# Building half of a scatter's key tiles one phase earlier, shares per phase for gathered rows, and ten whole blocks instead of six

## The chip, the cores and the metric

The kernel runs on one NeuronCore of a Trainium2 chip, as one launch. The metric is the device time of one execution in microseconds (us). Before the change the median of three runs is 2544.63 us (2541.19 to 2548.04).

## The reference, cut to what matters

Two layers of a hybrid decoder run over 256 prompt tokens and 64 sample tokens, in fp32 with 1024 features. The first half of a layer (retention and a recurrent branch) is not touched here. The second half is PEER: every token has eight heads, each head picks the best 16 of 128 x 128 experts by two lists of 128 keys, and each expert is one neuron.

```
q = (xf @ wq).reshape(n, 8, 2, 128);  s = einsum('nhpd,hpkd->nhpk', q, keys)
top_s, top_i = top_k(s, 16);  cand = top_s[:,:,0,:,None] + top_s[:,:,1,None,:]
best_s, best_c = top_k(cand.reshape(n, 8, 256), 16)
eidx = i1 * 128 + i2;  gate = softmax(best_s)          # 128 experts for each token
hid = gelu(einsum('nd,nkd->nk', x, u_tab[eidx])) * gate
out = einsum('nk,nkd->nd', hid, v_tab[eidx])
```

## The kernel before, in words

**Prompt tokens go through all 16384 experts as dense products.** A layer's expert half has eight phases of 32 items each, in the order U1, U0, U3, V1, U2, V0, V3, V2 (PHASES). The letter says which table is used and the digit which quarter of its 128 blocks. An item takes one block of 128 x 1024 fp32 numbers (512 KB), which SP loads into one of five `raw` buffers, five items ahead (`load`). `split`, two items ahead, has ACT round it to `hi` (L216) and DVE subtract to get `lo` (L218), in three buffers each, because a product is made as hi*hi + lo*hi + hi*lo in the fast fp32r format. A U item is 24 matmuls of 256 columns into PSUM, and after every second one a GELU into the SBUF tile `H`. A V item (`vmm`) is 12 matmuls of 512 columns that add to four PSUM banks held through all V phases. Its other operand is `H`, itself split by `hsplit` (L1146, L1147) once for two items. In V0 the items for which `whole` is true (i//2 in 3, 7, 11: six items) are not split. They multiply `raw` and `H` in plain fp32 (L1160), with four calls.

**The scatter turns the chosen experts into a dense weight on `H`.** It runs once for quarters 0 and 1 (f=0, during U3) and once for quarters 2 and 3 (f=1, during V0). Each time it takes 32 groups of eight tokens. A group needs a key tile `sA` (L1080: compare the first index with a ramp, 128 x 1024 in f16), a tile `sO` (L1083), a tile `sB` (L1085: times the gates), 16 matmuls of 64 columns (L1095, L1096) and one DVE operation on `H` (L1102). The scatter is a pipeline: step g builds group g, places group g-1 on TensorE and weighs group g-2. With f=0 each key tile is built and also stored to DRAM (`kept`), and with f=1 it is read back from there. `sA` has three buffers, `sB` and the PSUM bank two.

**Sample tokens take their experts by rows.** `sample()` gathers 64 row tiles of `peer_u` and then 64 of `peer_v` (one indirect DMA from POOL for each, L1223, 128 rows of 4 KB, 512 KB), in three buffers `g4`. DVE reduces or adds each one two steps later (L1232, L1246).

**The order is written out by generators.** `choose` (the top-16 work), `scatter` and `sample` yield a cost after each step. Twice in each item `background` adds half of the item's `budget` (TUNE["peer"], one number per phase) to a credit, and steps the queue `bg` until the credit is used up. Only what `bg` leaves goes to `bg2`, which holds `sample`. So in U3 and V0 rows are gathered when the scatter has ended, and in the other phases as fast as the budget allows (1.3 for a row). All five engines run their own instructions strictly in the order in which this program issues them, so a DVE instruction that waits for a gathered row holds up the next `lo`.

`phase` drains `choose` before U3 and a scatter before the V phase that needs it. `post_v2` drains what is left of both queues at item 28 of V2.

Of the kernel before, what the change touches and what calls it, by code (L numbers as in the profile page):

```python
# [12 lines left out]
F16 = mybir.dt.float16  # L13
# [4 lines left out]
OP = mybir.AluOpType  # L18
# [4 lines left out]
NPT = 256  # L23
# [27 lines left out]


TUNE = dict(gret=4.4, xr=3.6, grnn=1.6, ga=2.5, gb=3.1,
            peer=(1.45, 1.66, 2.5, 1.2, 1.2, 2.2, 1.2, 1.25))


class Background:
# [28 lines left out]
class Trunk:  # L86
# [134 lines left out]
    def run(self):  # L221
        self.items, self.blocks, self.raw, self.hl = [], [], {}, {}
        for l in range(self.depth):
            Layer(self, l).plan()
        self.credit = 0.0
        for k, it in enumerate(self.items):
            self.k = k
            if it.get("pre"):
                it["pre"]()
            self.split(k + 2)  # L230
            if not it["whole"]:
                self.load(k + RAWS)
            for _ in it["mm"](*self.hl.pop(k)):
                self.background(it, 0.5)
            if it["whole"]:
                self.load(k + RAWS)
            for f in self.late.pop(k, []):
                f()
            if it.get("post"):
                it["post"]()  # L240
            self.background(it, 0.5)
        self.final()

    def background(self, it, f):
        left = self.bg2.advance(self.bg.advance(self.credit + f * it["budget"]))
        self.credit = min(left, 0.0)

    def at(self, dk, f):
        self.late.setdefault(self.k + dk, []).append(f)
# [16 lines left out]
class Layer:  # L266
# [5 lines left out]
    def plan(self):  # L272
        T, a = self.T, self.a
        n0 = len(T.items)

        def add(mm, post=None, pre=None, lo="dve", budget=2.0, whole=False):
            T.items.append(dict(mm=mm, post=post, pre=pre, lo=lo, budget=budget, whole=whole))

        x = lambda: (T.xh, T.xl)
        pair = self.fm_pair(x)  # L280
        for c in range(8):
            add(pair[c] if c < 2 else self.fm(x), lambda c=c: self.post_qk(c), pre=self.start if c == 0 else None)
        for h in range(2):
            for kp in range(4):
                add(self.tm(x, h, kp), lambda h=h, kp=kp: self.post_v(h, kp))
        for c in range(8):
            add(self.fm(x), lambda c=c: self.post_gret(c), pre=self.start_ret if c == 0 else None, budget=TUNE["gret"])
        for c in range(8):
            add(self.fm(x), lambda c=c: self.post_xr(c), budget=TUNE["xr"])
        for c in range(8):  # L290
            add(self.fm(x), lambda c=c: self.post_grnn(c), pre=self.start_rgl if c == 0 else None, budget=TUNE["grnn"])
        for g in range(2):
            for c in range(8):
                add(self.fm(x), lambda g=g, c=c: self.post_gate(g, c), budget=TUNE[("ga", "gb")[g]])
        for c in range(8):
# [12 lines left out]
        for ph, (kind, q) in enumerate(PHASES):
            for i in range(PHB):
                e = q * PHB + i  # L310
                pre = (lambda kind=kind, q=q: self.phase(kind, q)) if i == 0 else None
                mm, post = (self.umm, self.post_u) if kind == "U" else (self.vmm, self.post_v2)
                add(mm(q, i), lambda post=post, q=q, i=i: post(q, i), pre=pre, budget=TUNE["peer"][ph],
                    whole=self.whole(kind, q, i))
                T.blocks.append(a["ut"][e] if kind == "U" else a["peer_v"].rearrange("(p j) d -> j p d", j=KEYS)[e])
        T.items[-1]["last"] = True
# [634 lines left out]
    def choose(self, t):  # L951
# [101 lines left out]
        T.at(3, turn)  # L1053
        yield 1.0

    def scatter(self, f):
        T, nc, pp = self.T, self.nc, self.pp
        ng = NPT // 8
        w2 = 2 * PHB
        st = {}  # L1060
        if f == 0:
            self.kept = [T.dp.tile([128, 1024], F16, tag=f"kept{g}", name="kept") for g in range(ng)]

        def v(t, g, w):
            pairs = t[:, g * 8:(g + 1) * 8].rearrange("p (a b) -> p a b", b=2)
            return pairs[:, :, None, :].to_broadcast([128, 4, w, 2])

        def ramp(k0, w):
            return T.iota_a[:, None, k0:k0 + w, :].to_broadcast([128, 4, w, 2])

        def fetch(g):
            A = st["A", g] = pp.tile([128, 4, 128, 2], F16, tag="sA", name="sA", bufs=3)
            if f:
                nc.sync.dma_start(A.rearrange("p a k b -> p (a k b)"), self.kept[g])

        def build(g):
            A = st.pop(("A", g))
            B = pp.tile([128, 2, 4, w2, 2], F16, tag="sB", name="sB", bufs=2)
            if f == 0:
                nc.vector.tensor_tensor(A, v(self.i1T, g, 128), ramp(0, 128), op=OP.is_equal)  # L1080
                nc.sync.dma_start(self.kept[g], A.rearrange("p a k b -> p (a k b)"))
            hot = pp.tile([128, 4, w2, 2], F16, tag="sO", name="sO")
            nc.vector.tensor_tensor(hot, v(self.i2T, g, w2), ramp(f * w2, w2), op=OP.is_equal)  # L1083
# [18 lines left out]
            nc.vector.scalar_tensor_tensor(hv, p, 1.0 / GSC, hv, op0=OP.mult, op1=OP.mult)  # L1102
            self.weighed[f] += 8

        if f:
            fetch(0)
        for g in range(ng + 2):
            while self.chosen < (1 if g < ng // 2 else 2):
                yield 2.0
            if g + f < ng:  # L1110
                fetch(g + f)
            if g < ng:
                build(g)
            if 0 <= g - 1 < ng:
                place(g - 1)
            if 0 <= g - 2 < ng:
                weigh(g - 2)
            yield 1.8 if f else 2.3

    def look_ahead(self, kind, q, i):  # L1120
        n = PHASES.index((kind, q)) + 1
# [26 lines left out]
            self.hid[q, i][2] = upto  # L1148

    def whole(self, kind, q, i):  # L1150
        return (kind, q) == ("V", 0) and i // 2 in (3, 7, 11)

    def vmm(self, q, i):
        nc, T = self.nc, self.T
# [250 lines left out]
```

## Time and profile before

| | before |
|---|---|
| median of 3 runs | 2544.63 us |
| profiled execution | 2543.64 us |
| its span | 2541.8 us |
| mean granted TensorE clock | 0.988 |
| expert half of layer 1, of layer 2 (to the end of V2) | 461.6 to 1267.9, 1728.0 to 2532.9 us |

Times below are from the span's start. Of a phase, the stretch runs from its first matmul to the first one of the next phase. Busy time is the time in which at least one instruction of the engine runs. On TensorE matmuls overlap, so a stretch with 100% is one in which it never stood still.

### The profile page before, as it was taken

How to read it: one execution, taken by the hardware profiler on the slowest of the kernel's cores; microseconds unless marked ns; L12 is line 12 of the kernel's file. 1: busy time of each engine (PE TensorE's matmuls, PEld its weight loads, DVE VectorE, ACT ScalarE, POOL GpSimd, SP SyncE). 2: the span in 40 equal slices, each digit the busy share in tenths (PEclk: the TensorE clock that was granted, in tenths of full speed). 3: DMA queues.
4: the chain of work that ended last, by engine and by line, in shares of the span. 5: the costliest groups of instructions: out<-in, count | busy, mean ns of one | idle time of the engine just before them, and what ended most of it. 6: DMA issues, size and time to landing. Idle time of an engine off the chain costs nothing. (4 is left out here: it accounts for less than half of the span.)

```text
span 2541.8 us, 42734 instructions
## 1 busy us (share of the span) xinstructions
PE 2422.8 (95%) x16588; PEld 2176.6 (86%) x16588; DVE 1955.1 (77%) x3503; ACT 1102.5 (43%) x1551; POOL 489.9 (19%) x305
## 2 busy tenths in 40 slices
PE   8989999999899999999999899999999999999998
PEld 7879899999898897777788798899998988977776
DVE  7465657887898878888764756588878998787896
ACT  4437344454334443344543363444543344433444
POOL 0000004002203540055000000040032045401550
PEclk9999999999999999999999999999999999999999
DMA  6333444456868997699652334445577689976994
GB/s 236 111 108 117 143 149 131 160 182 244 280 212 291 369 347 261 231 336 348 215 203 88 113 119 142 144 132 161 183 254 267 216 320 359 343 251 240 340 357 164
DMA packets 169899, 563.27 MB, mean 222 GB/s; under 512 B 20321, under 2 KB 27489, under 8 KB 168929
## 3 DMA queue, kind: packets, MB, share of 16 engines
q1 hardware_dynamic: 130960, 419.15, 48.8%
q0 software_dynamic: 36864, 134.23, 14.0%
q10 hardware_dynamic: 1872, 7.16, 0.7%
q8 instruction: 130, 2.13, 0.3%
q14 instruction: 73, 0.59, 0.1%
HBM read 537.37 MB, written 23.10 MB: 221 GB/s over the span
## 5 line engine op out<-in xcount | busy, mean ns | idle before, releaser
L216 ACT CAST hi<-raw 128x1024 fp32r<-128x1024 f32 x692 | 725.2, 1048 | 694.4 <-PE ps_acc L1179 432.7
L218 DVE TENSOR_TENSOR lo<-raw,hi 128x1024 fp32r<-128x1024 f32 x668 | 813.4, 1220 | 269.0 <-ACT hi L216 264.8
L938 PE MATMUL ps_h<-xh,lo 128*128 128x256 f32 x2048 | 583.3, 285 | 20.6 <-DVE lo L218 20.6
L936 PE MATMUL ps_h<-xh,hi 128*128 128x256 f32 x2048 | 587.6, 287 | 0.0
L937 PE MATMUL ps_h<-xl,hi 128*128 128x256 f32 x2048 | 581.4, 284 | 0.0
L938 PEld LDWEIGHTS ps_h<-xh,lo 128*128 128x128 f32 x2048 | 394.9, 193 | 24.1 <-DVE lo L218 24.0
L1178 PE MATMUL ps_acc<-lo,hh 128*128 128x512 f32 x976 | 383.7, 393 | 16.3 <-DVE lo L218 16.3
L937 PEld LDWEIGHTS ps_h<-xl,hi 128*128 128x128 f32 x2048 | 395.2, 193 | 0.1
L936 PEld LDWEIGHTS ps_h<-xh,hi 128*128 128x128 f32 x2048 | 395.1, 193 | 0.1
L1179 PE MATMUL ps_acc<-hi,hl 128*128 128x512 f32 x976 | 384.2, 394 | 2.2 <-DVE hl L1147 0.4
L1177 PE MATMUL ps_acc<-hi,hh 128*128 128x512 f32 x976 | 385.9, 395 | 0.0
L1223 POOL DMA_INDIRECT g<-in_peer_u,eS x128 | 205.5, 1605 | 703.6 <-DVE g L1232 412.3
L350 PE MATMUL ps_acc<-xh,hi 128*128 128x320 f32 x960 | 309.3, 322 | 3.0 <-ACT hi L216 3.0
L352 PE MATMUL ps_acc<-xh,lo 128*128 128x320 f32 x960 | 300.8, 313 | 8.4 <-DVE lo L218 8.4
L351 PE MATMUL ps_acc<-xl,hi 128*128 128x320 f32 x960 | 299.6, 312 | 0.0
L1223 POOL DMA_INDIRECT g<-in_peer_v,eS x128 | 205.4, 1605 | 404.9 <-DVE xs L1246 373.2
L1178 PEld LDWEIGHTS ps_acc<-lo,hh 128*128 128x128 f32 x976 | 183.8, 188 | 63.1 <-DVE lo L218 26.4
L1179 PEld LDWEIGHTS ps_acc<-hi,hl 128*128 128x128 f32 x976 | 183.6, 188 | 48.6 <-DVE hl L1147 11.1
L1177 PEld LDWEIGHTS ps_acc<-hi,hh 128*128 128x128 f32 x976 | 183.8, 188 | 36.1 <-issue 0.5
L1232 DVE SCALAR_TENSOR_TENSOR g<-g,xs 128x1024 f32<-128x1024 f32 x128 | 156.2, 1223 | 63.4 <-DMA g<-in_peer_u,eS 62.5
L946 ACT ACTIVATE H<-ps_h 128x512 f32<-128x512 f32 x128 | 76.5, 598 | 277.7 <-PE ps_h L938 277.6
L352 PEld LDWEIGHTS ps_acc<-xh,lo 128*128 128x128 f32 x960 | 183.0, 191 | 11.1 <-DVE lo L218 11.0
(284 smaller groups left out, 3436.2 us busy)
## 6 DMA issues: line engine op xcount, KB each, us to landing
raw<-in_ut SPq DMA_DIRECT2D x256, 512.0 KB
raw<-in_peer_v SPq DMA_DIRECT2D x256, 512.0 KB
raw<-in_wall SPq DMA_DIRECT2D x192, 512.0 KB
kept<-sA SPq DMA_DIRECT2D x64, 256.0 KB
sA<-kept SPq DMA_DIRECT2D x64, 256.0 KB
r<-in_r0t SPq DMA_DIRECT2D x2, 2048.0 KB
out_sr_s<-r ACTq DMA_DIRECT2D x2, 2048.0 KB
aux<-in_c_mP SPq DMA_DIRECT2D x16, 192.0 KB
```

What stands on the lines that cost most here:

```text
L216: nc.scalar.copy(hi, raw)
L218: eng.tensor_tensor(lo, raw, hi.bitcast(F32), op=OP.subtract)
L350: nc.tensor.matmul(o, wh, xh[:, k, :], start=k == 0, stop=False)
L351: nc.tensor.matmul(o, wh, xl[:, k, :], start=False, stop=False)
L352: nc.tensor.matmul(o, wl, xh[:, k, :], start=False, stop=k == 7)
L936: nc.tensor.matmul(o, uh, xh, start=k == 0, stop=False, skip_group_check=True)
L937: nc.tensor.matmul(o, uh, xl, start=False, stop=False, skip_group_check=True)
L938: nc.tensor.matmul(o, ul, xh, start=False, stop=k == 7, skip_group_check=True)
L1177: nc.tensor.matmul(self.acc[t][d], hh[:, s], hi[:, c], start=first, stop=False)
L1178: nc.tensor.matmul(self.acc[t][d], hh[:, s], lo[:, c], start=False, stop=False)
L1179: nc.tensor.matmul(self.acc[t][d], hl[:, s], hi[:, c], start=False, stop=last)
L1223: nc.gpsimd.indirect_dma_start(out=g, out_offset=None, in_=T.a[tab].rearrange("l e d -> (l e) d"), in_offset=bass.IndirectOffsetOnAxis(ap= ...
```

## The change

1. `keys_ahead`, a new generator behind `choose` in `bg`, builds the key tiles of groups 0 to 15 and stores them, as soon as half of the tokens are chosen. That is in U0, at a cost of 0.75 for each.
2. `scatter(0)` reads these 16 tiles back from DRAM like `scatter(1)` does. A tile is fetched one step ahead in both. A step costs 1.8 where the tile is read and 2.5 where it is built (2.3 before).
3. `sample` gets credits of its own, TUNE["rows"], one number per phase. In U1 and U0 it gets at most what `bg` has left.
4. The budgets of U3, V0 and V2 go from 2.5 to 2.35, 2.2 to 1.95 and 1.25 to 1.2.
5. `whole` is true for i//2 in 2, 5, 8, 11, 14: ten items of V0 instead of six.

```diff
-            peer=(1.45, 1.66, 2.5, 1.2, 1.2, 2.2, 1.2, 1.25))
+            peer=(1.45, 1.66, 2.35, 1.2, 1.2, 1.95, 1.2, 1.2),
+            rows=(0.5, 1.5, 0.0, 1.1, 1.17, 0.62, 1.08, 1.26))
...
     def background(self, it, f):
-        left = self.bg2.advance(self.bg.advance(self.credit + f * it["budget"]))
+        left = self.bg.advance(self.credit + f * it["budget"])
         self.credit = min(left, 0.0)
+        rows = f * it["rows"]
+        if it["after"]:
+            rows = min(max(left, 0.0), rows)
+        self.credit2 = min(self.bg2.advance(self.credit2 + rows), 0.0)
...
-                add(..., budget=TUNE["peer"][ph],
+                add(..., budget=TUNE["peer"][ph], rows=TUNE["rows"][ph], after=ph < 2,
...
                 self.chooser = [T.bg.add(self.choose(t)) for t in (2, 0, 1)][-1]
+                T.bg.add(self.keys_ahead())
                 T.bg2.add(self.sample())
...
+    def key_hot(self, A, g):
+        nc = self.nc
+        nc.vector.tensor_tensor(A, self.by_pairs(self.i1T, g, 128), self.ramp(0, 128), op=OP.is_equal)
+        nc.sync.dma_start(self.kept[g], A.rearrange("p a k b -> p (a k b)"))
+
+    def keys_ahead(self):
+        self.kept = [self.T.dp.tile([128, 1024], F16, tag=f"kept{g}", name="kept") for g in range(NPT // 8)]
+        while not self.chosen:
+            yield 0.5
+        for g in range(NPT // 16):
+            self.key_hot(self.key_tile(), g)
+            yield 0.75
...
+        stored = lambda g: f or g < ng // 2
         def fetch(g):
-            A = st["A", g] = pp.tile([128, 4, 128, 2], F16, tag="sA", name="sA", bufs=3)
-            if f:
-                nc.sync.dma_start(A.rearrange("p a k b -> p (a k b)"), self.kept[g])
+            if g < ng:
+                A = st["A", g] = self.key_tile()
+                if stored(g):
+                    nc.sync.dma_start(A.rearrange("p a k b -> p (a k b)"), self.kept[g])
...
-            if f == 0:
-                nc.vector.tensor_tensor(A, v(self.i1T, g, 128), ramp(0, 128), op=OP.is_equal)
-                nc.sync.dma_start(self.kept[g], A.rearrange("p a k b -> p (a k b)"))
+            if not stored(g):
+                self.key_hot(A, g)
...
-        if f:
-            fetch(0)
+        fetch(0)
...
-            if g + f < ng:
-                fetch(g + f)
+            fetch(g + 1)
...
-            yield 1.8 if f else 2.3
+            yield 1.8 if stored(g) else 2.5
...
-        return (kind, q) == ("V", 0) and i // 2 in (3, 7, 11)
+        return (kind, q) == ("V", 0) and i // 2 in (2, 5, 8, 11, 14)
```

## Rows read from the trace of the kernel before

**Rows 1.** The page: busy time, share of the span and instructions of each engine.

```profile
PE 2422.8 (95%) x16588; PEld 2176.6 (86%) x16588; DVE 1955.1 (77%) x3503; ACT 1102.5 (43%) x1551; POOL 489.9 (19%) x305
```

**Rows 2.** Windows by phase. Layer 1 (eight), layer 2 (U0, U3, V1), sum of all sixteen.

```profile
core 0: us, PE busy (x) PEld busy (x) DVE busy (x) ACT busy (x) POOL busy (x), PEclk, DMA share, GB/s
461.60:558.00 96.40, 93.69 (x780) 93.31 (x779) 83.55 (x261) 46.36 (x57) 0.00 (x0) 1.00 0.54 175
558.00:659.30 101.30, 95.27 (x775) 94.45 (x775) 80.07 (x170) 47.84 (x60) 28.71 (x19) 0.98 0.72 253
659.30:780.60 121.30, 112.37 (x1282) 109.16 (x1281) 114.12 (x170) 41.64 (x49) 5.04 (x3) 1.00 0.70 233
780.60:871.60 91.00, 88.88 (x386) 71.83 (x386) 80.75 (x108) 42.32 (x49) 49.74 (x30) 1.00 0.93 340
871.60:963.80 92.20, 92.20 (x770) 92.19 (x769) 71.53 (x77) 41.48 (x49) 39.55 (x29) 1.00 0.96 349
963.80:1078.50 114.70, 110.62 (x874) 80.96 (x873) 94.05 (x139) 34.55 (x40) 6.58 (x5) 1.00 0.69 237
1078.50:1175.30 96.80, 91.08 (x385) 72.70 (x384) 84.98 (x81) 42.03 (x48) 52.66 (x32) 0.98 0.95 339
1175.30:1267.90 92.60, 89.93 (x385) 71.35 (x383) 70.90 (x68) 44.13 (x53) 22.99 (x13) 1.00 0.76 267
...
1824.30:1924.50 100.20, 95.35 (x777) 94.54 (x776) 79.59 (x170) 47.85 (x60) 28.88 (x19) 0.98 0.74 253
1924.50:2048.20 123.70, 114.59 (x1282) 111.56 (x1281) 114.87 (x170) 41.62 (x49) 5.04 (x3) 0.97 0.68 231
2048.20:2136.00 87.80, 87.62 (x386) 71.97 (x385) 80.52 (x108) 42.34 (x49) 47.95 (x30) 1.00 0.95 351
...
sum 1611.20, PE 1549.42 PEld 1373.00 DVE 1362.05 ACT 680.25 POOL 411.39; mean PE 96.84 PEld 85.81 DVE 85.13 ACT 42.52 POOL 25.71
```

**Rows 3.** Windows: U3 items 2 to 7 and 13, V0 items 14 and 15.

```profile
671.29:691.97 20.68, 20.68 (x246) 20.42 (x243) 20.06 (x31) 6.96 (x9) 0.00 (x0) 1.00 0.75 258
710.20:715.96 5.76, 4.26 (x58) 3.86 (x57) 5.69 (x11) 2.58 (x3) 0.00 (x0) 1.00 0.52 182
...
1016.21:1024.20 7.99, 7.99 (x55) 3.98 (x51) 7.74 (x12) 1.27 (x2) 0.00 (x0) 1.00 0.76 234
```

**Rows 4.** DVE's groups: count, busy us, mean ns, idle us before them and releasers.

```profile
L218 DVE TENSOR_TENSOR lo<-raw,hi 128x1024 fp32r<-128x1024 f32 x668 | 813.4, 1220 | 269.0 <-ACT hi L216 264.8
...
L1246 DVE SCALAR_TENSOR_TENSOR xs<-g,cS,xs 128x1024 f32<-128x1024 f32 x126 | 161.6, 1282 | 38.8 <-DMA g<-in_peer_v,eS 37.2 <-DVE hl L1147 0.3
L1232 DVE SCALAR_TENSOR_TENSOR g<-g,xs 128x1024 f32<-128x1024 f32 x128 | 156.2, 1223 | 63.4 <-DMA g<-in_peer_u,eS 62.5
L1085 DVE TENSOR_TENSOR sB<-sO,gg 128x1024 f16<-128x1024 f16 x128 | 88.7, 693 | 15.7 <-PE ps_m L1096 5.3 <-PE ps_h L938 0.5
L1102 DVE SCALAR_TENSOR_TENSOR H<-ps_m,H 128x512 f32<-128x512 f32 x128 | 87.5, 684 | 0.0
L1147 DVE TENSOR_TENSOR hl<-H,hh 128x512 fp32r<-128x512 f32 (+1 forms) x124 | 83.8, 676 | 0.0
...
L1083 DVE TENSOR_TENSOR sO<-i2T,iota_a 128x512 f16<-128x512 f16 x128 | 53.6, 418 | 0.1
L1080 DVE TENSOR_TENSOR sA<-i1T,iota_a 128x1024 f16<-128x1024 f16 x64 | 43.8, 684 | 0.0
```

**Rows 5.** Timeline of DVE and PE in U0, item 25: start us, us, idle before.

```profile
631.31 1.23 DVE L1232 SCALAR_TENSOR_TENSOR g<-g,xs 128x1024 f32<-128x1024 f32 x1 [3.00 <-DMA g<-in_peer_u,eS]
...
633.74 0.39 PE L938 MATMUL ps_h<-xh,lo 128*128 128x256 f32 x1 [2.47 <-DVE lo L218]
```

**Rows 6.** Windows: first two late items of V3 (layers 1, 2), then steady V3.

```profile
1081.25:1094.15 12.90, 7.87 (x25) 5.56 (x24) 9.70 (x11) 2.61 (x3) 6.39 (x4) 0.87 0.79 272
2346.82:2357.37 10.55, 6.29 (x26) 4.35 (x24) 8.07 (x9) 2.61 (x3) 5.29 (x4) 1.00 0.79 280
...
1090.00:1130.00 40.00, 39.90 (x168) 32.42 (x168) 36.59 (x36) 16.82 (x19) 21.20 (x13) 0.96 0.98 351
```

More of the change, by code (lines that the diff above doesn't have):

```diff
@@ L224, in run @@
             Layer(self, l).plan()
-        self.credit = 0.0
+        self.credit = self.credit2 = 0.0
         for k, it in enumerate(self.items):
@@ L274, in plan, with add @@
         n0 = len(T.items)
-        def add(mm, post=None, pre=None, lo="dve", budget=2.0, whole=False):
-            T.items.append(dict(mm=mm, post=post, pre=pre, lo=lo, budget=budget, whole=whole))
+        def add(mm, post=None, pre=None, lo="dve", budget=2.0, rows=0.0, after=False, whole=False):
+            T.items.append(dict(mm=mm, post=post, pre=pre, lo=lo, budget=budget, rows=rows, after=after,
+                                whole=whole))
         x = lambda: (T.xh, T.xl)
@@ L312, in plan @@
                 mm, post = (self.umm, self.post_u) if kind == "U" else (self.vmm, self.post_v2)
-                add(mm(q, i), lambda post=post, q=q, i=i: post(q, i), pre=pre, budget=TUNE["peer"][ph],
+                add(mm(q, i), lambda post=post, q=q, i=i: post(q, i), pre=pre, budget=TUNE["peer"][ph], rows=TUNE["rows"][ph], after=ph < 2,
                     whole=self.whole(kind, q, i))
@@ L1054, in choose, with by_pairs, ramp, key_tile @@
         yield 1.0
+    def by_pairs(self, t, g, w):
+        pairs = t[:, g * 8:(g + 1) * 8].rearrange("p (a b) -> p a b", b=2)
+        return pairs[:, :, None, :].to_broadcast([128, 4, w, 2])
+    def ramp(self, k0, w):
+        return self.T.iota_a[:, None, k0:k0 + w, :].to_broadcast([128, 4, w, 2])
+    def key_tile(self):
+        return self.pp.tile([128, 4, 128, 2], F16, tag="sA", name="sA", bufs=3)
+    def key_hot(self, A, g):
[9 more added lines that the diff above has]
+            yield 0.75
     def scatter(self, f):
@@ L1060, in scatter @@
         st = {}
-        if f == 0:
[L1062 to L1069, printed above, removed]
+        stored = lambda g: f or g < ng // 2
         def fetch(g):
-            A = st["A", g] = pp.tile([128, 4, 128, 2], F16, tag="sA", name="sA", bufs=3)
-            if f:
-                nc.sync.dma_start(A.rearrange("p a k b -> p (a k b)"), self.kept[g])
+            if g < ng:
+                A = st["A", g] = self.key_tile()
+                if stored(g):
+                    nc.sync.dma_start(A.rearrange("p a k b -> p (a k b)"), self.kept[g])
         def build(g):
@@ L1078, in build @@
             B = pp.tile([128, 2, 4, w2, 2], F16, tag="sB", name="sB", bufs=2)
[L1079 to L1081 removed]
+            if not stored(g):
+                self.key_hot(A, g)
             hot = pp.tile([128, 4, w2, 2], F16, tag="sO", name="sO")
[L1083 removed]
+            nc.vector.tensor_tensor(hot, self.by_pairs(self.i2T, g, w2), self.ramp(f * w2, w2), op=OP.is_equal)
             gates = self.gg[:, g].rearrange("p s (a b) -> p (s a) b", b=2)
```

## The prediction

> **What bounds the kernel now.** I read the page's busy line first: TensorE (PE) works 95% of the span, DVE 77% [rows 1]. So the floor is PE's work, and only what each phase takes above it can be won. Next come the windows by phase [rows 2]. U2 shows the bare price of a U item: PE never stands still, 92.20 us / 32 = 2.88. The second layer's V1 gives a V item: 87.80 / 32 = 2.74. U3's steady items with one scatter group take 20.68 / 6 = 3.45 [rows 3], so a group costs PE 0.57. Two whole items with a group each take 7.99 [rows 3], so a whole item is 4.00 - 0.57 = 3.43, which is 0.69 more than a split one.
>
> The floors follow. U1, U0 and U2 take 92.2 each; U3 takes 92.2 + 32 x 0.57 = 110.4; V1, V3 and V2 take 87.7 each; V0 takes 26 x 2.74 + 6 x 3.43 + 18.2 = 110.0. They add to 760.1 for a layer. Layer 1's eight rows add to 806.3, and the sum row leaves 804.9 for layer 2 [rows 2]. So the expert halves stand 46.2 and 44.8 us above their floors. In layer 1 this excess is, in order, U1 4.2, U0 9.1, U3 10.9, V1 3.3, U2 0.0, V0 4.7, V3 9.1, V2 4.9; in layer 2 U0 has 8.0, U3 13.3 and V1 0.1 [rows 2]. I read three causes.
>
> - U3: DVE is busy 114.1 of 121.3 us, more than PE's floor. An item with two groups takes 5.76 us, with DVE busy 5.69 of it and PE 4.26 [rows 3]. DVE's load sets that item.
> - U0's end: rows are gathered at 1.66 / 1.3 = 1.28 per item. DVE waits 3.00 us for a row, and the next `lo` reaches PE 2.47 us late [rows 5]. The lag is carried into U3. The granted clock is 0.98 there and 0.97 in layer 2's U3 [rows 2], after PE stood still; that part of the excess goes with the waits.
> - V3's first two late items take 12.90 and 10.55 us where 5.48 is the price [rows 6]: 7.4 and 5.1 of V3's excess. When V0's scatter ends, the old rule throws its leftover credit of 2.2 per item at rows, 1.7 per item.
>
> Besides, V1, U2 and V3 hold the transfers at shares of 0.93 to 0.96 and 339 to 351 GB/s [rows 2]; V3's steady stretch has 0.98 and 351 [rows 6]. I take 351 as the ceiling. A row and a block are 0.524 MB each, so 0.92 rows per V item ask for 1.92 x 0.524 / 2.74 = 367 GB/s.
>
> **The change, part by part, for one layer.** First where things land, counted from the yields. `choose` costs 18.7 + 24.4 + 24.4 = 67.5 credits. U1 gives 42 and U0's first 15 items the rest. Sixteen keys at 0.75 then take 7 items, and the last 9 items of U0 get about 10 rows (19 POOL operations before [rows 2]). U3's scatter asks 16 x 1.8 + 18 x 2.5 = 73.8 of its 75.2. Rows become: U3 0 (before 3), V1 27 (30), U2 27 (29), V0 15 (5), V3 27 (32), V2 22 (13).
>
> *U0.* DVE gains 16 key builds, 16 x 0.684 = 10.9 us, and loses 9 rows, 9 x 1.22 = 11.0 [rows 4]: nothing net. While keys are built an item holds 2.2 x 0.684 + 1.22 = 2.7 us of DVE against 2.88 of PE, so PE hides them. SP gets 16 stores earlier, each behind its build, with the block loads queued behind it; the five `raw` buffers cover that. The fourth key must wait for the first one's store. If it lands within 3 us this costs nothing. If it took as long as a row's round trip (three steps at the 3 us spacing of V3's rows, 96.8 / 32 [rows 2]) a key would take 3 us, and 16 keys 48 us against 20 of PE: up to +28. A key tile is half a block, sent without POOL, so I take 0.5. Rows then come at 1.15 per item, asking 2.15 x 0.524 / 2.88 = 391 GB/s, a lag of 0.33 us per item, 3 us over 9 items. The old 1.28 asks 415, 0.52 per item, and reached PE only at the tenth such item [rows 5], so 5 us of lag are absorbed. Excess 9.1 -> 2.0 (1 to 6).
>
> *U3.* DVE loses 10.9 us of builds and 3 rows (3.7): 114.1 -> 99.5, below PE's 110.4. By item: the durations of rows 4 add to 3.70 for a built group and a `lo`, but DVE's busy time is 20.06 / 6 = 3.34 [rows 3], so overlap takes 10%. With stored keys, 1.31 groups per item are 0.9 x (1.22 + 1.31 x 1.80) = 3.2 of DVE against 2.88 + 1.31 x 0.57 = 3.62 of PE; in the built half, 3.2 against 3.42. What is late next is PE itself. Still, four items have two stored groups, 4.3 of DVE against 4.02. Added: 16 reads of 256 KB. SP's read of g+1 waits until PE has placed g-2, with a block load behind it; V0 runs this pattern already, and its whole excess is 4.7. From below the excess is 1, from above 7 (V0's, and a start that still carries U0's lag). I take 3.0, nearest to V0 without its double start. 10.9 -> 3.0.
>
> *V0.* Four more whole items: 4 x 0.69 = +2.8 on PE. DVE loses 4 x 1.22 + 2 x 0.68 = 6.2 and gains 10 rows x 1.28 = 12.8 [rows 4]: 94.0 -> 100.7, against a floor of 112.8. A split item now has 0.9 x (1.22 + 0.34 + 1.80 + 0.48 x 1.28) = 3.6 of DVE against 3.31 of PE, a whole one 2.2 against 4.0. Four split and two whole make 18.8 against 21.2, if DVE can use the whole pair's slack for the next four. I take an excess of 4.0 (1.5 to 12) after 4.7: +2.1 in all.
>
> *V3.* The start burst is gone. 0.83 rows per item ask for 350 GB/s, just the ceiling. 9.1 -> 2.5 (1 to 6). *V1* likewise, 3.3 -> 1.5. *U2* 0.5.
>
> *V2.* 22 rows at 0.97 ask 377 GB/s: 2.94 us per item, 0.20 x 23 = 4.6. The old 13 rows at 0.96 cost 4.9. I take 4.5 (2 to 10). `sample` now ends at item 27, its output at the drain of item 28; the last four items (11 us) hide that.
>
> U1 4.2 stays. Sum of the excess: 4.2 + 2.0 + 3.0 + 1.5 + 0.5 + 4.0 + 2.5 + 4.5 = 22.2, and 2.8 for whole items: 25.0 against 46.2 and 44.8. That is -21.2 and -19.8, together -41.0.
>
> The profiled execution took 2543.64 us (span 2541.8), one below the median 2544.63. 2543.6 - 41.0 = 2502.6, or 2503 on the median's scale.
>
> The Trainium skill ("DMA: Bandwidth & Descriptors", section Bandwidth) has a core that streams alone reach about 425 GB/s, and about 358 as its share when its neighbour streams too. The rows stop at 351 with shares of 0.95 to 0.98, so here the lower figure agrees. By the higher one 377 would fit, and the time would be that of rival C.
>
> **Rivals.**
> - A. V0 turns DVE-bound. Its slack in the whole pairs can't be saved up: 22 split items x 0.3 = 6.6, and 4 for its double groups, instead of 4.0. For: strict order and two or three buffers everywhere. Against: the old whole pairs ran 7.99 without a gap. +6.6 x 2: 2516.
> - B. The excess goes with the rows. The same 128 rows are fetched; what left U0 and V3 (7.1 + 6.6) comes back in V0 and V2, and only U3's 7.9 less 2.8 is won: 5.1 x 2 = 10: 2533. For: V2 pays 4.9 for 13 rows. Against: U2 takes 29 rows for nothing.
> - C. 351 GB/s was what was asked, not a ceiling. Then V3, V1 and V2 fall to about 1 each: -5.5 x 2: 2492. Against: the share of 0.98.
> - D. Slower. Rows now stand in DVE's queue between scatter steps, and each wait stops both `lo` and `sB`. V0 has 112.8 - 100.7 = 12.1 us of DVE slack. If each of its 13 uses waits 2.6 us or more (34 us), V0 grows by 22 and the gain is gone; at rows 5's 3.00 us it is 39 - 12 = +27 per layer, 2503 + 54 = 2557. Against: V0's rows are nearly 8 us apart, so three steps are 23 us, and the round trip is 9.
> - E. The stores hold the keys back (+28 in U0, above): 2559 at the end, 2515 if a key takes 1.7 us instead of 1.31.
>
> **How the numbers follow.** Forecast with its own range 2490 to 2515: 0.64. A 0.10, B 0.08, C 0.08, D 0.05, E 0.05. The range to 8 in 10 reaches to C's side at 2487 and past A to 2526; B, D and the far end of E stay out. A measurement of this kernel can tell 0.3% (7.6 us) from no change. Faster holds the forecast, A, C, nearly all of B and E's near end: 0.91. Same, 0.04, is where B and D go halfway; slower, 0.05, D and E's end.
>
> **What would show it.** Right: U3 near 113 with DVE under 102 busy and no two-group item above 4.6; no wait for a row in U0's items 23 to 31; V3's first three items at 2.7 to 3.3; V0 near 117 with eight more PE calls per pair of whole items; V2 about as long as before. Wrong: V0 above 122 with DVE at 95% (A), V2 or V0 longer by what U0 and V3 lose (B), windows above 360 GB/s (C), DVE waiting for rows inside V0's scatter (D), builds in U0 spaced over 1.6 us (E).

## The result, and the profile after

The changed kernel takes 2511.22 us (median of 4 runs, 2506.02 to 2518.14), the kernel before 2543.19 (4 runs, 2541.19 to 2548.04): a ratio of 0.9879 with a 95% interval of 0.9856 to 0.9902. The forecast was 2503, with a range of 2487 to 2526. The profiled execution took 2508.14 us (before 2543.64), with a span of 2506.4.

The page's first line answers to [rows 1]: DVE has 12 instructions fewer, and PE's busy share rose from 95.3 to 96.5% because the span shrank.

```profile
PE 2419.1 (97%) x16556; PEld 2175.8 (87%) x16556; DVE 1943.1 (78%) x3491; ACT 1092.6 (44%) x1539; POOL 485.4 (19%) x305
```

The windows by phase answer to [rows 2], in the same order: the eight phases of layer 1 (U1, U0, U3, V1, U2, V0, V3, V2), then layer 2's U0, U3, V1, V0, V3 and V2, then the sum over all sixteen.

```profile
core 0: us, PE busy (x) PEld busy (x) DVE busy (x) ACT busy (x) POOL busy (x), PEclk, DMA share, GB/s
463.80:561.60 97.80, 95.09 (x779) 94.71 (x778) 83.57 (x261) 46.36 (x57) 0.00 (x0) 0.98 0.53 173
561.60:656.40 94.80, 93.41 (x776) 92.95 (x775) 77.51 (x166) 48.03 (x60) 13.29 (x9) 1.00 0.75 259
656.40:778.10 121.70, 114.25 (x1282) 111.57 (x1282) 104.71 (x151) 41.83 (x49) 3.36 (x2) 0.97 0.67 227
778.10:865.90 87.80, 87.70 (x386) 71.97 (x385) 75.54 (x99) 42.02 (x48) 43.43 (x26) 1.00 0.92 329
865.90:958.10 92.20, 92.20 (x770) 92.19 (x769) 73.48 (x93) 41.36 (x48) 42.28 (x30) 1.00 0.97 361
958.10:1072.00 113.90, 113.37 (x857) 78.18 (x857) 100.39 (x147) 29.56 (x36) 17.55 (x14) 1.00 0.82 289
1072.00:1159.00 87.00, 87.00 (x385) 72.06 (x384) 77.55 (x75) 42.08 (x48) 42.51 (x25) 1.00 0.92 333
1159.00:1249.10 90.10, 88.77 (x385) 71.40 (x384) 81.37 (x78) 44.24 (x53) 38.43 (x23) 1.00 0.90 328
...
1808.10:1903.00 94.90, 93.54 (x776) 92.99 (x775) 77.34 (x165) 48.10 (x60) 13.52 (x9) 1.00 0.74 256
1903.00:2025.70 122.70, 113.82 (x1283) 110.99 (x1282) 104.76 (x151) 41.82 (x49) 3.73 (x3) 0.97 0.67 227
2025.70:2112.70 87.00, 87.00 (x386) 72.04 (x385) 76.47 (x99) 42.04 (x48) 44.43 (x26) 1.00 0.94 337
...
2204.90:2318.80 113.90, 113.37 (x858) 78.21 (x857) 100.38 (x147) 29.57 (x36) 17.55 (x14) 1.00 0.82 293
2318.80:2405.90 87.10, 87.10 (x386) 72.09 (x385) 78.56 (x75) 42.07 (x48) 43.88 (x26) 1.00 0.92 332
2405.90:2497.50 91.60, 89.57 (x385) 71.46 (x383) 81.53 (x85) 43.74 (x57) 39.50 (x24) 1.00 0.82 302
sum 1571.00, PE 1541.98 PEld 1368.19 DVE 1349.65 ACT 670.56 POOL 406.99; mean PE 96.37 PEld 85.51 DVE 84.35 ACT 41.91 POOL 25.44
```

The sum fell from 1611.20 to 1571.00, by 40.2 us; the forecast was 41.0. The rest of the span runs the same code and took 2506.4 - 1571.0 = 935.4 us, against 930.6. That rest lies between 926 and 935 in this case's traces, so I read nothing into its +4.8; it is why the profiled execution gained only 35.5. By the medians the gain is 32.0.

That the sum came out is luck: U3 missed by 17.6 us over the two layers, and the other phases together came out better by nearly as much. This is the excess over the prediction's floors, in us, each phase's duration less its floor:

| phase | forecast | layer 1 | layer 2 |
|---|---|---|---|
| U1 | 4.2 | 5.6 | 4.1 |
| U0 | 2.0 | 2.6 | 2.7 |
| **U3** | **3.0** | **11.3** | **12.3** |
| V1 | 1.5 | 0.1 | -0.7 |
| U2 | 0.5 | 0.0 | 0.0 |
| V0 (ten whole items) | 4.0 | 1.1 | 1.1 |
| V3 | 2.5 | -0.7 | -0.6 |
| V2 | 4.5 | 2.4 | 3.9 |
| sum | 22.2 | 22.4 | 22.8 |

Two of the floors were a little off. V3's items now take 2.72 us each, so 32 of them take 87.0 us and not 87.7, which is why some excesses are below zero. And U0 takes 93.1 where PE never stands still in it (the run with spaced keys, below), 0.9 above its floor of 92.2.

U3, from which the forecast wanted 8 to 10 us a layer, gave +0.4 and -1.0. Its windows below show why. They are the first item, the end of that item after the last wait of PE, an item with two stored groups (item 8), 12 us of the stored half, and an item with one built group (item 15). In the first, PE worked 5.38 of 9.38 us, at a granted clock of 0.75, where an item's price is 3.45. In layer 2 that item took 10.60. Behind the windows stand two timelines of the start, DVE's and then PE's (start us, us, and in brackets the idle time before and what ended it).

```profile
656.45:665.83 9.38, 5.38 (x42) 5.07 (x41) 7.83 (x11) 1.53 (x2) 3.36 (x2) 0.75 0.96 348
662.30:665.83 3.53, 3.53 (x28) 3.53 (x28) 2.11 (x3) 0.00 (x0) 0.00 (x0) 0.50 1.01 370
692.76:698.03 5.27, 4.08 (x58) 3.86 (x57) 3.48 (x7) 2.58 (x3) 0.00 (x0) 1.00 0.65 225
...
672.00:684.00 12.00, 12.00 (x148) 11.83 (x147) 10.08 (x15) 3.63 (x4) 0.00 (x0) 1.00 0.66 230
...
719.53:723.40 3.87, 3.61 (x42) 3.40 (x41) 3.84 (x7) 1.05 (x1) 0.00 (x0) 1.00 0.64 207
```

```profile
653.68 1.23 DVE L1252 SCALAR_TENSOR_TENSOR g<-g,xs 128x1024 f32<-128x1024 f32 x1 [2.30 <-DMA g<-in_peer_u,eS]
656.34 1.23 DVE L1252 SCALAR_TENSOR_TENSOR g<-g,xs 128x1024 f32<-128x1024 f32 x1 [1.43 <-DMA g<-in_peer_u,eS]
657.49 1.22 DVE L219 TENSOR_TENSOR lo<-raw,hi 128x1024 fp32r<-128x1024 f32 x1
658.81 1.23 DVE L1252 SCALAR_TENSOR_TENSOR g<-g,xs 128x1024 f32<-128x1024 f32 x1
659.97 1.22 DVE L219 TENSOR_TENSOR lo<-raw,hi 128x1024 fp32r<-128x1024 f32 x1
661.11 0.42 DVE L1105 TENSOR_TENSOR sO<-i2T,iota_a 128x512 f16<-128x512 f16 x1
661.56 0.69 DVE L1107 TENSOR_TENSOR sB<-sO,gg 128x1024 f16<-128x1024 f16 x1
```

```profile
658.77 0.39 PE L945 MATMUL ps_h<-xh,lo 128*128 128x256 f32 x1 [1.92 <-DVE lo L219]
...
662.30 0.21 PE L1117 MATMUL ps_m<-sB,sA 128*128 128x64 f16 x1 [2.07 <-DVE sB L1107]
...
697.55 0.19 PE L1117 MATMUL ps_m<-sB,sA 128*128 128x64 f16 x1 [1.19 <-DVE H L1124]
```

DVE waits 2.30 and 1.43 us for U0's last rows. Behind them stand two `lo` and the first group's `sO` and `sB`, so PE loses 1.92 us to a late `lo` and 2.07 to a late `sB`: 4.0 us. The window at 0.75 shows the other part: PE's work there took 5.38 us for 3.45. The last row of the timelines is of item 8. There PE waits 1.19 us for the DVE operation on `H` (L1124), which empties a PSUM bank and stands in DVE's queue behind the next `sO` and `sB`. DVE is busy only 3.48 of this item's 5.27 us, so it is its order that makes this item late, and not its load.

Two more places answer to the forecast. V0 takes 14 POOL operations, and DVE never waits for a row inside it. V3's first items, 12.90 and 10.55 us for two late ones before [rows 6], now run at their price. These are its first two items in layer 1:

```profile
1072.00:1074.72 2.72, 2.72 (x13) 2.25 (x12) 1.52 (x3) 1.57 (x2) 0.00 (x0) 1.00 0.63 236
1074.72:1077.44 2.72, 2.72 (x13) 2.25 (x12) 2.72 (x4) 1.05 (x1) 0.81 (x1) 1.00 0.49 194
```

### The profile page after: what moved, and what is told of

Read it like the earlier page. It is cut to its first block, busy times and chain, and to the rows that moved or that the text cites. A ratio compares the mean times of both kernels' runs of the same rounds, so it can differ in the third digit from the quotient of the medians.

```text
span 2506.4 us, 42676 instructions
## 1 busy us (share of the span) xinstructions
PE 2419.1 (97%) x16556; PEld 2175.8 (87%) x16556; DVE 1943.1 (78%) x3491; ACT 1092.6 (44%) x1539; POOL 485.4 (19%) x305
## 5 line engine op out<-in xcount | busy, mean ns | idle before, releaser
L217 ACT CAST hi<-raw 128x1024 fp32r<-128x1024 f32 x684 | 717.0, 1049 | 686.9 <-PE ps_acc L1199 393.4
L219 DVE TENSOR_TENSOR lo<-raw,hi 128x1024 fp32r<-128x1024 f32 x660 | 803.2, 1221 | 270.1 <-ACT hi L217 267.2
L1197 PE MATMUL ps_acc<-hi,hh 128*128 128x512 f32 x944 | 373.8, 396 | 0.0
L1198 PE MATMUL ps_acc<-lo,hh 128*128 128x512 f32 x944 | 368.4, 390 | 2.7 <-DVE lo L219 2.7
L1199 PE MATMUL ps_acc<-hi,hl 128*128 128x512 f32 x944 | 369.0, 391 | 0.7
L1198 PEld LDWEIGHTS ps_acc<-lo,hh 128*128 128x128 f32 x944 | 177.4, 188 | 41.7 <-DVE lo L219 5.3
L1199 PEld LDWEIGHTS ps_acc<-hi,hl 128*128 128x128 f32 x944 | 177.2, 188 | 41.3 <-DVE hl L1167 4.4
L1197 PEld LDWEIGHTS ps_acc<-hi,hh 128*128 128x128 f32 x944 | 177.3, 188 | 36.1 <-issue 1.4
L356 PEld LDWEIGHTS ps_acc<-xh,hi 128*128 128x128 f32 x960 | 183.9, 192 | 10.3 <-ACT hi L217 5.0
```

The costliest lines, as they stand in the source:

```text
L217: nc.scalar.copy(hi, raw)
L219: eng.tensor_tensor(lo, raw, hi.bitcast(F32), op=OP.subtract)
L356: nc.tensor.matmul(o, wh, xh[:, k, :], start=k == 0, stop=False)
L1197: nc.tensor.matmul(self.acc[t][d], hh[:, s], hi[:, c], start=first, stop=False)
L1198: nc.tensor.matmul(self.acc[t][d], hh[:, s], lo[:, c], start=False, stop=False)
L1199: nc.tensor.matmul(self.acc[t][d], hl[:, s], hi[:, c], start=False, stop=last)
```

## The experiments

Each ratio is to the kernel before, run beside it on the same chip, with its 95% interval. "U3 115.6 | 115.6" gives layer 1 and layer 2. The diffs are against the changed kernel.

### No rows in U0: is U3's late start U0's lag?

```diff
-            rows=(0.5, 1.5, 0.0, 1.1, 1.17, 0.62, 1.08, 1.26))
+            rows=(0.0, 0.0, 0.0, 1.1, 1.17, 1.0, 1.08, 1.26))
```

> The changed kernel's U3 begins with an item of 9.4 and 10.6 us where 3.45 is the price. Here U0 gathers no rows, and V0's share goes from 0.62 to 1.0 (25 rows instead of 15). Theory 1 (DVE enters U3 late because it waited for rows at U0's end): U3's first item falls to 4.6 or less, U3 from 122 to about 115.5 us, U0 to 93.5, so -8 us per layer there; V0 then has 100.4 + 11 x 1.28 = 114 us of DVE work against 113.9 of TensorE, and grows by 3 to 10 us per layer: 2500 to 2512 in all. Rival (cold start: the first groups wait for the first tiles read back, whatever the rows do): U3 stays at 121 to 122, V0 grows all the same: 2515 to 2530.

Measured: 0.9852 (0.9812 to 0.9892), 2500.67 us. U0 95.7 | 95.8, U3 115.6 | 115.6, V0 117.2 | 117.2. The windows are of layer 1's U3 and V0:

```profile
655.60:771.10 115.50, 111.46 (x1282) 108.93 (x1281) 99.63 (x144) 41.83 (x49) 0.00 (x0) 1.00 0.65 215
...
950.30:1067.50 117.20, 113.84 (x858) 78.28 (x857) 110.02 (x165) 29.55 (x36) 29.99 (x23) 1.00 0.91 323
```

U3's first item takes 3.45 us, and the phase is 6 to 7 us shorter. So the late start is the lag of U0's rows, not a start of the scatter from cold. DVE's 99.63 in U3 is the forecast's 99.5: its 104.7 in the changed kernel was work left over from U0. The rows that V0 takes instead (23 operations of POOL for 14) cost 3.3 there, with DVE at 110.0. U0 is still 2.6 us above 93.1, late at items 22 to 25, though no rows are left: the wait there is that of a key for its buffer (7.1 us of DVE in four waits in layer 1).

### Six whole items instead of ten

```diff
-        return (kind, q) == ("V", 0) and i // 2 in (2, 5, 8, 11, 14)
+        return (kind, q) == ("V", 0) and i // 2 in (3, 7, 11)
```

> The changed kernel with six whole items in V0 as before (i//2 in 3, 7, 11). Theory (whole items buy DVE time that the rows in V0 need): TensorE's work in V0 falls by 4 x 0.69 = 2.8 us, DVE's rises by 6.2 to 106.6 against a floor of 110, and V0 comes out at 114 to 119 us instead of 113.9, 2511 to 2521 in all. Rival (the four more whole items were not needed): V0 falls to 111 to 112, 2506 in all.

Measured: 0.9858 (0.982 to 0.9897), 2505.96 us. V0 112.1 | 113.7, with DVE busy 105.6: 1.8 and 0.2 us less than with ten. The four added whole items are not needed for 15 rows in V0. The whole times can't be told apart: the interval holds the changed kernel's 0.9879.

### No keys ahead

```diff
-            peer=(1.45, 1.66, 2.35, 1.2, 1.2, 1.95, 1.2, 1.2),
-            rows=(0.5, 1.5, 0.0, 1.1, 1.17, 0.62, 1.08, 1.26))
+            peer=(1.45, 1.66, 2.5, 1.2, 1.2, 1.95, 1.2, 1.2),
+            rows=(0.5, 0.78, 0.0, 1.1, 1.17, 0.62, 1.08, 1.26))
...
-                T.bg.add(self.keys_ahead())
+                self.kept = [T.dp.tile([128, 1024], F16, tag=f"kept{g}", name="kept") for g in range(NPT // 8)]
...
-        stored = lambda g: f or g < ng // 2
+        stored = lambda g: f
...
-            yield 1.8 if stored(g) else 2.5
+            yield 1.8 if stored(g) else 2.3
```

> The changed kernel without the key tiles ahead: all 32 are built in U3 (budget 2.5, step 2.3, as before), and U0's rows are thinned to 0.78 per item over its second half, about 10 rows as in the changed kernel. Theory (the keys take 10.9 us off DVE in U3, but the late start at U0's end takes it back): U3 keeps the old kernel's steady excess of 5.9 us without its late start, 117 to 119 us, less than the changed kernel's 122; 2501 to 2506 in all. Rival (the keys ahead are worth their full 8 us per layer and the start is the same without them): U3 at 126 to 130, 2520 to 2530.

Measured: 0.9837 (0.9796 to 0.9878), 2498.6 us. U0 93.1 | 93.1, U3 117.0 | 117.0. The window is layer 1's U3:

```profile
655.50:772.50 117.00, 111.91 (x1283) 108.92 (x1282) 108.14 (x161) 41.88 (x49) 0.32 (x1) 1.00 0.67 226
```

U3 builds all 32 keys itself, DVE is 3.4 us busier than in the changed kernel, and the phase is still 4.7 and 5.7 us shorter. Its first item takes 3.37. In U0 the rows come from its middle on (0.78 per item), and DVE never waits for one. This run takes out the keys and thins the rows, so by itself it does not say which of the two mends the start; a run below keeps the keys beside rows as thin as these, and there DVE is late again.

### Even steps in the scatter of U3

```diff
-            yield 1.8 if stored(g) else 2.5
+            yield 1.8 if f else 2.3
```

> The changed kernel with a cost of 2.3 for every step of the first scatter, read or built, so that nearly every item of U3 has one group and none has two. Theory (an item with two stored groups is set by DVE: 4.7 and 5.3 us against 4.02): the double items of the changed kernel (5, 8, 11) and its four items of 3.87 go, U3 falls by 3 to 4.5 us, 2503 in all. Rival (these stalls only pay for work that DVE must do in U3 anyway, and reappear elsewhere): U3 the same within 1 us, 2510.

Measured: 0.9855 (0.9815 to 0.9895), 2503.01 us. U3 120.3 | 119.9, or -1.4 and -2.8. The items with two groups in the stored half (4.68, 5.28 and 4.68 us in the changed kernel) are gone, but one of 5.76 stands at item 29, and six items with one built group take 3.87 (items 17 to 27), where the changed kernel had four. The whole fall lies in the first item (7.90 and 7.09, for 9.38 and 10.60), and why it fell is open. The rest of U3 takes 112.4 | 112.8, against 112.3 | 112.1, so in the rest of the phase the rival holds: what the double items gave up came back. That the time is the 2503 of the theory says little, since the kernel before took 2536.22 beside it.

### One part alone: the shares, then the keys

The shares alone are the kernel of the third experiment with six whole items:

```diff
-        return (kind, q) == ("V", 0) and i // 2 in (2, 5, 8, 11, 14)
+        return (kind, q) == ("V", 0) and i // 2 in (3, 7, 11)
```

> One part of the change alone: rows have shares of their own per phase (V0's budget 1.95, V2's 1.2), but all keys are built in U3 (budget 2.5, step 2.3) and six items of V0 are whole. U0's rows run at 0.78 over its second half. Theory (the shares carry the whole gain, keys ahead and ten whole items are worth nothing together): U0 93, U3 117, V0 112 to 114, V3 87, ratio to before 0.982 to 0.986. Rival (the parts need each other: six whole items can't carry the rows in V0 and built keys hold U3): V0 above 117 or U3 above 120, ratio 0.988 or more.

Measured: 0.9823 (0.9797 to 0.9849), 2496.27 us. U0 93.1, U3 117.0, V0 114.5 | 113.7, V3 87.5 | 87.8. The interval lies below that of the changed kernel, so the shares alone beat all three parts together. They are not quite the change's own, since U0's rows go at 0.78 per item and not at 1.5 behind the keys; no run has 1.5 without keys.

The keys ahead alone have the budgets, the joint background and the six whole items of the kernel before:

```diff
-            peer=(1.45, 1.66, 2.35, 1.2, 1.2, 1.95, 1.2, 1.2),
+            peer=(1.45, 1.66, 2.5, 1.2, 1.2, 2.2, 1.2, 1.25),
...
-        left = self.bg.advance(self.credit + f * it["budget"])
+        left = self.bg2.advance(self.bg.advance(self.credit + f * it["budget"]))
...
-        rows = f * it["rows"]
-        if it["after"]:
-            rows = min(max(left, 0.0), rows)
-        self.credit2 = min(self.bg2.advance(self.credit2 + rows), 0.0)
...
-        return (kind, q) == ("V", 0) and i // 2 in (2, 5, 8, 11, 14)
+        return (kind, q) == ("V", 0) and i // 2 in (3, 7, 11)
```

> Another part alone: 16 key tiles are built ahead in U0 and read back, but rows take what is left over, with the budgets and six whole items of before. Theory (the stores and the rows together make DVE late at U0's end, so the keys' 10.9 us are lost to U3's start): U3 stays at 119 to 124, V3 at 96 to 97, U0 at 96 to 100: 0 to 8 us less than before in all. Rival (moving keys is worth its 8 us per layer by itself): U3 at 113 to 115, 16 us less.

Measured: 0.9989 (0.9972 to 1.0006), 2540.52 us. U0 97.0 | 95.6, U3 123.8 | 125.4 (first item 9.66 and 11.07), V3 98.5 | 96.0. The window is layer 1's U3:

```profile
656.50:780.30 123.80, 114.63 (x1283) 111.54 (x1282) 105.61 (x155) 41.87 (x49) 6.39 (x5) 0.97 0.66 227
```

The shares, with U0's rows thinned, carry the whole gain. The keys took 8.5 us of DVE out of U3 (114.1 to 105.6) and moved the time by nothing that can be measured: U0 gained 4.4 and 4.6 us, and V0 3.3 and 3.6, but U3 lost 2.5 and 1.7 and V1 1.0 and 6.3.

### Two ways to part the rows from the keys in U0

First the rows at 0.78 per item beside the keys, from the end of the choice on:

```diff
-            rows=(0.5, 1.5, 0.0, 1.1, 1.17, 0.62, 1.08, 1.26))
+            rows=(0.5, 0.78, 0.0, 1.1, 1.17, 0.62, 1.08, 1.26))
...
-            rows = min(max(left, 0.0), rows)
+            rows = 0.0 if self.chooser is None or self.chooser in self.bg.q else rows
```

> The changed kernel with U0's rows spread thin (0.78 per item) beside the key builds, from the end of the top-16 work on, instead of dense (1.5) in the last nine items. Theory P (transfers: U0's second half asks 17 blocks, 16 stores and 10 rows, 18.3 MB in 49 us, 374 GB/s, more than the 351 to 356 seen anywhere): DVE is late all the same, U3's first item 6 us or more. Theory Q (only the dense rows at the end were too fast for their round trip): U3's first item 4.6 or less, U3 115.6, U0 at most 96: 6 us per layer less than the changed kernel, ratio 0.983.

Measured: 0.9857 (0.9823 to 0.989), 2506.65 us. The windows are layer 1's U0 and U3:

```profile
562.80:664.30 101.50, 96.71 (x776) 95.76 (x775) 82.41 (x173) 48.19 (x60) 15.54 (x11) 0.97 0.75 257
664.30:780.10 115.80, 111.67 (x1282) 108.98 (x1281) 99.69 (x144) 41.83 (x49) 0.37 (x1) 1.00 0.67 225
```

Neither theory held as I wrote it. U3 starts nearly on time (3.69 and 4.24), but U0's items 21 to 26 are late, one of them takes 7.90 us: the lag is paid where it arises (U0 101.5 | 97.3). With the same rows and no keys U0 took 93.1, and with the keys and no rows 95.7, so it takes both to make DVE this late.

Then the keys at 1.6 credits instead of 0.75, in the kernel without rows in U0:

```diff
-            yield 0.75
+            yield 1.6
```

> The kernel with keys ahead and no rows in U0 (V0's share 1.0), with the sixteen key builds spaced at 1.6 instead of 0.75, about one per item to U0's end. Theory (at 2.2 keys per item the three key buffers wait for their stores to land, and DVE is late by 1 to 2 us at items 22 to 25): U0 falls from 95.7 to 93.1 to 93.5, U3 stays at 115.6. Rival (those stalls come from loads of blocks held up on SP behind the stores): U0 stays above 94.5.

Measured: 0.9851 (0.9811 to 0.9891), 2501.38 us. The window is layer 1's U0, with U3 117.2 | 117.3:

```profile
561.00:654.10 93.10, 93.10 (x777) 92.89 (x776) 73.61 (x157) 47.91 (x60) 5.45 (x3) 1.00 0.68 234
```

With keys spaced out PE never stands still in U0. Its late items at 22 to 25 were the keys' wait for their three buffers. But the last key now falls at U0's end, and U3's first item takes 5.09 us: PE waits there 1.48 us for the first key tile to be read back (DMA `sA<-kept`).

### One group per item

Keys in U3, six whole items, shares as before, and each step's cost equal to the budget of an item:

```diff
-            peer=(1.45, 1.66, 2.35, 1.2, 1.2, 1.95, 1.2, 1.2),
-            rows=(0.5, 1.5, 0.0, 1.1, 1.17, 0.62, 1.08, 1.26))
+            peer=(1.45, 1.66, 2.5, 1.2, 1.2, 1.8, 1.2, 1.2),
+            rows=(0.5, 0.78, 0.0, 1.1, 1.17, 0.62, 1.08, 1.26))
...
-                T.bg.add(self.keys_ahead())
+                self.kept = [T.dp.tile([128, 1024], F16, tag=f"kept{g}", name="kept") for g in range(NPT // 8)]
...
-        stored = lambda g: f or g < ng // 2
+        stored = lambda g: f
...
-            yield 1.8 if stored(g) else 2.5
+            yield 1.8 if stored(g) else 2.5  # as the budgets
...
-        return (kind, q) == ("V", 0) and i // 2 in (2, 5, 8, 11, 14)
+        return (kind, q) == ("V", 0) and i // 2 in (3, 7, 11)
```

> The shares alone, and every scatter step costs just what an item's budget is (2.5 in U3, 1.8 in V0), so that each item has one group, in its second half, and none has two. Theory (with shares and an even scatter U3 is within 2 us of TensorE's own work): no item of 5.76 and fewer of 3.87, U3 111 to 113 instead of 117, V0 110 to 112, 0.5 more at the start of V1 and V3: 4 to 6 us per layer less than the shares alone, ratio 0.979 to 0.982. Rival (the built groups' DVE work of 114 us comes due in U3 whatever its order): U3 116 to 118.

Measured: 0.9771 (0.9739 to 0.9804), 2480.76 us. U3 110.2 | 110.2, V0 111.2 | 111.4. The windows are layer 1's U3 and V0:

```profile
653.00:763.20 110.20, 110.20 (x1282) 108.82 (x1281) 106.43 (x160) 41.95 (x50) 0.33 (x1) 1.00 0.70 233
...
943.40:1054.60 111.20, 110.30 (x875) 80.84 (x873) 103.31 (x149) 34.46 (x41) 17.60 (x13) 1.00 0.87 301
```

PE does not stand still once in U3: 110.20 of 110.20, although DVE is busy 106.43, more than in the changed kernel. DVE's total was not what held U3 back; uneven steps were. In the third experiment, with the same 32 keys built in U3, two items with two groups (5.76 and 5.80 us) and seven with one (3.85 to 3.98) make up 6.2 of the 6.6 us above the floor. PE's wait in both is for the DVE operation on `H`. These are all of PE's waits in layer 1's U3, first with the shares alone, then in the kernel without rows in U0 (us, times, longest):

```profile
PE ps_m L1117 <- DVE H L1124: 5.1, 10, 1.7
...
PE ps_m L1117 <- DVE H L1124: 4.0, 8, 1.2
```

With one group per item this wait is gone, and U3 and V0 together are 10.1 and 9.1 us shorter than with the shares alone.

### The whole items again, on the even scatter

```diff
-        return (kind, q) == ("V", 0) and i // 2 in (3, 7, 11)
+        return (kind, q) == ("V", 0) and i // 2 in (2, 5, 8, 11, 14)
```

This one, like the next, is against the kernel with one group per item.

> The even scatter of the run before (keys built in U3, one group per item, row shares) with ten whole items in V0 instead of six. Theory (with an even scatter DVE is not short in V0, so a whole item only costs TensorE its 0.69 us): V0 from 111.3 to 114.0 us, 2.7 per layer, ratio 0.979 to 0.980. Rival (the stall of 1 us at V0's start and the slower start of V3, 89.1, come from DVE, which ten whole items relieve): V0 and V3 together no longer than with six, ratio 0.976 to 0.977.

Measured: 0.9763 (0.9728 to 0.9798), 2481.26 us. V0 113.8 | 114.7 (+2.6 and +3.3), V3 87.2 | 87.2 (-1.9). The price of 2.8 that the prediction put on four whole items is there, and V3 gives part of it back. In the whole time the two kernels can't be told apart.

```diff
-        return (kind, q) == ("V", 0) and i // 2 in (3, 7, 11)
+        return (kind, q) == ("V", 0) and i // 2 in ()
```

> The even scatter with no whole item at all. Theory (whole items pay where DVE is the bound): TensorE's work in V0 falls by 6 x 0.69 = 4.1 us to 107, but DVE's rises from 103 to 103 + 6 x 1.22 + 3 x 0.68 = 112.4, so V0 is set by DVE at 112 to 116, against 111.3 with six. Rival (DVE's lead of nearly two items is enough): V0 107 to 109, ratio 0.974.

Measured: 0.9825 (0.9786 to 0.9864), 2496.02 us. The window is layer 1's V0:

```profile
941.30:1057.60 116.30, 108.41 (x899) 84.94 (x897) 112.21 (x158) 42.33 (x50) 17.84 (x14) 1.00 0.82 287
```

With no whole item DVE works 112.2 of 116.3 us, and from item 11 on nearly every second item takes 4.1 to 4.2. So V0 does need some whole items, and six are enough; no run has fewer of them.

### The best version: fewer rows in V2

Against the kernel with one group per item:

```diff
-            rows=(0.5, 0.78, 0.0, 1.1, 1.17, 0.62, 1.08, 1.26))
+            rows=(0.5, 0.78, 0.0, 1.15, 1.22, 0.72, 1.13, 1.1))
```

> The even scatter with V2's rows slowed from 1.26 to 1.1 per item and the others raised a little (V1 1.15, U2 1.22, V0 0.72, V3 1.13), so that V2 has about 14 rows instead of 22. Theory (V2 asks 377 GB/s at 0.97 rows per item, and its 4.7 and 5.9 us above the price are waits for rows): V2 falls by 2 to 4 us per layer, V1, U2 and V3 rise by at most 1 each, ratio 0.974 to 0.977. Rival (rows cost about the same wherever they are): V1, U2 and V3 rise by what V2 gains, ratio 0.977.

Measured: 0.9719 (0.9684 to 0.9755), 2471.78 us. V2 88.9 | 89.7, and 770.8 and 770.6 us for the expert halves, against 785.3 and 785.6 in the changed kernel. The window is layer 1's V2:

```profile
1148.70:1237.60 88.90, 88.46 (x385) 71.59 (x383) 75.25 (x72) 44.15 (x53) 30.33 (x17) 1.00 0.84 302
```

It beats the kernel before and the changed kernel. Against the kernel with one group per item, to which its edit was made, V2 falls by 2.9 and 3.4 us and an expert half by 2.6 and 2.8, but the two ratios' intervals overlap, so the whole time does not show this step. Most of V2's late items go when its rows do.

## Why the prediction was right in its sum and wrong in a step

*U0: right in size, wrong in what became of it.* An excess of 2.0 was forecast; it is 2.6 and 2.7, of which 0.9 is the floor's error. The prediction let its lag end there ("5 us of lag are absorbed"), and this failed. Here are the sixteen key builds of layer 1's U0 (ns, first and last start in us), the waits of DVE before them, and its waits before the rows up to U3's first item (us, times):

```profile
L1075 DVE TENSOR_TENSOR sA<-i1T,iota_a x16: 681/686/694, 609.3 to 634.5; 128x1024 f16<-128x1024 f16 x16
...
  DMA kept<-sA: 6.4, 6
...
  DMA g<-in_peer_u,eS: 4.4, 4
```

The builds wait 6.4 us for the stores of earlier keys, because at 1.66 / 0.75 = 2.2 keys per item the three buffers come round sooner than the stores land. That was rival E's mechanism; I priced it at 0.5, and E's sign came: the builds are 25.2 / 15 = 1.68 us apart, over 1.6. The rows that come behind the keys are late as well. At 0.524 MB per block and row, ten rows in nine items ask more (391 GB/s in the prediction) than the transfers gave there: 367 GB/s, at a share of 1.01. That the transfers were full is read from this share; no run tests it by itself.

```profile
647.00:656.40 9.40, 9.40 (x81) 9.40 (x80) 5.52 (x9) 3.63 (x4) 4.29 (x3) 1.00 1.01 367
```

In U0 PE lost only 1.7 and 1.8 us to all this (94.8 and 94.9 against 93.1); DVE went into U3 late, and there PE had to wait for it.

*U3: the failed step.* Its term was 3.0 with a top of 7 ("a start that still carries U0's lag"); it measured 11.3 and 12.3. The start is 9.38 - 3.45 = 5.9 and 10.60 - 3.45 = 7.2 of it. It goes when U0's rows go (3.45 in the first experiment), and when the keys go and the rows are thinned (3.37 in the third). The other 5.4 and 5.1 are uneven steps. The kernel without rows in U0 has this part alone: 115.6 - 110.4 = 5.2. Its four items with two stored groups take 4.68, 4.68, 5.28 and 4.68. I had put their DVE work at 4.3 us against PE's 4.02, and at 4.02 they stand 3.2 us too high. Four items with one built group take 3.87 for 3.45, another 1.7, and these eight items hold all of PE's waits there (4.0 us, eight times, for the operation on `H`); here I had DVE at 3.2 against PE's 3.42 and expected nothing. The kernel with one group per item has neither part: 110.2.

The wrong reading stood at the start: "DVE's load sets that item" [rows 3] is true of the old item with two built groups, and I carried it to the phase and to the items with stored groups. In those of 4.68 us DVE is nearly always busy too, but in the longest only 3.48 of 5.27 us, and in PE's waits all of them look alike. What was missing is PE's wait for the DVE operation on `H`, which comes and goes with where in an item the step falls. The cure that I costed was less DVE work; what helped was the same work spread evenly.

*V0: forecast too dear.* 4.0 of excess was forecast, 1.1 came. No row's wait stands in it, so rival D fell, and A with it: DVE was busy 100.39, forecast 100.7. That the four whole items cost 2.8 was right (2.6 and 3.3 on the even scatter); what they were to buy was not needed.

*V3: right, and better.* 9.8 and 10.0 us went, of which 6.6 were forecast. The burst had 7.4 and 5.1 of it [rows 6]; the rest went with later waits, in a phase that now takes 25 and 26 rows for 32. V1 and U2 were also at their price.

*V2: right.* It was to stay about as long with nine rows more; it took 90.1 and 91.6, 2.5 and 0.1 less than before, with ten more. One reading in it failed: the last four items do not hide the drain at item 28, which takes 4.57 and 4.54 us, 1.8 more than its price. In the best version moving some rows elsewhere gives 1 to 2 us of V2 back.

*Rivals and signs.* B fell: the rows that left U0 and V3 cost little where they went. C held in part: U2 runs at 361 GB/s without a gap on PE, so 351 was no ceiling. V1 and V3 stand at their price, but with fewer rows (329 to 337 GB/s), so they do not test it. The kernel before had already run past 351, in layer 2's V2:

```profile
2441.00:2481.00 40.00, 39.30 (x170) 31.30 (x169) 36.35 (x34) 18.37 (x21) 21.59 (x13) 1.00 0.97 361
```

Of the signs, three that were to show the forecast right did not come: U3 near 113, no wait for a row at U0's end, and V0 near 117. The one on PE's calls had its direction wrong. A pair of whole items has eight records fewer than a split pair, not more: the page's count fell by 32 for eight more whole items in two layers. No rival named the even scatter, which on top of the shares takes the ratio from 0.9823 to 0.9771, some 13 us. Their intervals just touch, but the slowest run of the one (2491.48) is below the fastest of the other (2494.62), and U3 and V0 show where it comes from.

## What to carry to other kernels

When work is moved ahead, ask what it waits for where it lands (here three buffers whose stores must land) and which queue carries that lag into the next stage, whose first item may have no slack at all. Make the cost of a background step equal to the budget of an item, so that each item carries the same at the same place: here an engine at 97% of a stage was no limit once no item went over. Before a costly rearrangement, try its cheap part alone: here the shares, with U0's rows thinned, gave 0.9823, and all three parts 0.9879.

## What the runs showed of the hardware that was not expected

The transfers go above the 351 GB/s that the prediction took as a ceiling. In this stretch of V2 in the changed kernel they run at 363 for 40 us with a share of 1.00, and PE has no gap:

```profile
1160.00:1200.00 40.00, 40.00 (x178) 32.93 (x177) 36.55 (x36) 19.22 (x23) 23.17 (x14) 1.00 1.00 363
```

The Trainium skill ("DMA: Bandwidth & Descriptors", section Bandwidth) gives about 425 GB/s for a core alone and about 358 as its share when its neighbour streams too. The rows lie just above the lower figure, which was no ceiling here; no run shows the higher one.

A stop of PE cost more than its length: 4.0 us of waiting at U3's start made the item 5.9 us longer. The granted clock of that item is 0.75, a mix of the full 2.4 GHz and the lower 1.2 GHz. After the second wait, from 662.30 to 665.83, it is 0.50, the lower level, and PE works without a gap.
